# Phase tables for eight pairs at a time, five input buffers, T4 by one difference, output units in two kinds of banks

## The chip, the cores and the metric

The kernel runs on one core of a Trainium2 chip. The metric is the time of one execution in microseconds of the device. The core has five engines with a queue of instructions each, which they run in order: TensorE (PE: matmuls and transposes), VectorE (DVE), ScalarE (ACT), GpSimd (POOL) and SyncE (SP, which here only issues DMAs). An instruction waits until all that it needs is there, and all behind it on its engine wait with it.

## The reference

One layer on x of shape (1, 2048, 1024), float32:

```python
h = rms_norm(x, norm_g)
proj = einsum('bsd,dc->bsc', h, w_in)             # 10240 columns
(ssm_u, ssm_gate, ret_q, ret_k, ret_v, ret_gate, diff_q, diff_k, diff_v, diff_gate,
 mem_q, mem_gate, merge) = split(proj)             # 12 pieces of 512, merge 4 x 1024
a_out = s5_branch(ssm_u, ...) * silu(ssm_gate)     # diagonal complex state, 32 groups
b_out = retention_branch(ret_q, ret_k, ret_v, ...) * silu(ret_gate)
c_out = diff_attn_branch(diff_q, diff_k, diff_v, ...) * silu(diff_gate)
m_out = memory_branch(mem_q, rms_norm(mem, mem_norm_g), ...) * silu(mem_gate)
br = einsum('bsnc,ncd->bsnd', stack(a_out, b_out, c_out, m_out), w_branch)
merged = sum(sigmoid(merge + b_merge) * br, axis=branch)
out = x + einsum('bsd,de->bse', merged, w_out)
```

In the S5 branch a state of group g runs with a = exp((lr + i li) dt), where dt = exp(log_dt).

## The kernel before

The 2048 tokens are two blocks b of 1024. In each block the stages follow one another: retention (32 units of a head and a token tile), differential attention, `projections`, `merge_output` (merging, the memory branch, the S5 output) and `output`. A float32 product is made of three: each factor is split into a high and a low half, x = xh + xl (names that end in h and l), and xh wh, xl wh and xh wl are summed in one bank of PSUM. A high half is a cast on ACT, a low half a subtraction on DVE or POOL. Apart from `projections`, whose order is written out by hand, a scheduler arranges the instructions of a stage for every engine, led by the due times with which code is put in (`ev.at`), and then each engine keeps that order.

**Input tiles** (`Norm`, L560 to L590). A tile of 128 tokens is loaded (`n_x`, L569), scaled (`n_junk` on ACT, `rms_m` on DVE, `rms_r` on POOL, `n_x` on DVE, L579) and transposed in two halves (PE, L586), then split into `xh` and `xl`. Block 0 has three buffers for it. Tiles 0 and 1 go first, the other six stand beside the first retention units, and the loads of the small parameter vectors (`vst`, `gqk`, `ldt_r`, `lt`) between them.

**S5 tables** (`setup_s5`, L308 to L440). Alongside retention of block 0, for four of 16 pairs of groups at a time (four blocks j0), the powers a^1 to a^128 are built by doubling (`tab`, products in `big`), brought to magnitude one and stored (`mats_d`). Then follow the matrices `gm` (transposed by PE at L372), `ca` (L426) and `tpad`. Retention's own instructions on DVE, `rsm` (L923: masked scores) and the rotations `ram` and `rbm`, stand in the same queue. The generator is advanced in 198 slots, one for each `yield`.

**T4** (`x_mix`, L1382 to L1407). `projections` multiplies by a scheme of seven products s instead of eight for a pair of column blocks (a `Pair`), on combinations of the four quarters of the block's input: T1, T2, T3 and T4 = B(0, 1) - T2, each for k = 0..3 and each split. Product s has 12 matmuls (L1355) into bank "abcbadc"[s]; `prepare` makes the weights' combinations and splits (`p_h`, `p_l`) ahead of it, and `collect` (`p_t`) takes banks over on DVE or ACT. T4 is used by product 5, and formed during products 0 to 3 of the first pair (`late`).

**Output** (L1543 to L1575). 16 units of 24 matmuls: `o = ps_mm()`, a bank of a pool of two; the sum with x (`mg_t`, L1572) releases it. The units' left factors `w1h` and `w1l` are eight pieces of 128x128 for each token tile.

Of the kernel before, what the change touches and what calls it, by code (L numbers as in the profile page):

```python
# [11 lines left out]
F32 = mybir.dt.float32  # L12
# [8 lines left out]
D = 1024  # L21
# [22 lines left out]
def trunk_kernel(ctx, tc, a):  # L44
# [135 lines left out]
    def setup_s5(p):  # L180
# [127 lines left out]
        dT = p.tile([16, 32], F32, name="dT")  # L308
        V.tensor_copy(dT, pt[0:16, 0:32])
        m = 4  # L310
        for j0 in range(0, n, m):
            yield
            js = slice(j0, j0 + m)
            big = [p.tile([128, m * 9 * 16], F32, name=f"big{i}") for i in range(2)]

            tab = p.tile([128, m, 2, 128], F32, name="tab")
            V.tensor_copy(tab[:, :, 0, 0], e_r[:, js])
            V.tensor_copy(tab[:, :, 1, 0], e_i[:, js])
            for q in (1, 2, 4, 8, 16, 32, 64):
                tmp = [bg[:, 0:m * q].rearrange("p (j c) -> p j c", j=m) for bg in big]  # L320
                cmul(tab[:, :, 0, q:2 * q], tab[:, :, 1, q:2 * q],
                     (tab[:, :, 0, 0:q], tab[:, :, 1, 0:q]),
                     (bc(tab[:, :, 0, q - 1], 2, q), bc(tab[:, :, 1, q - 1], 2, q)), tmp)
                yield
            tmp = [bg[:, 0:m * 128].rearrange("p (j c) -> p j c", j=m) for bg in big]
            tt(tmp[1], tab[:, :, 1, :], tab[:, :, 1, :], ALU.mult, G)
            yield
# [50 lines left out]
                DMA.dma_start(out=mats_d[:, j0 + j:j0 + j + 2, 0:256], in_=ev)  # L378
                yield

            cm = p.tile([16, 2, 2 * m, 64], F32, name="cm")
            for i, nm in enumerate(("ssm_c_re", "ssm_c_im")):
                DMA.dma_start(out=cm[:, i], in_=a[nm][0].rearrange("g h p -> h g p")[:, 2 * j0:2 * j0 + 2 * m, :])
            cT = p.tile([128, 2, m, 16], F32, name="cT")
# [31 lines left out]
                                  in_=ca[r0:r0 + 64, i, :, 1:9, :].rearrange("p j s h -> p j (s h)"))  # L416
                yield

            tpad = p.tile([16, m, 2, 256], F32, name="tpad")
            V.memset(tpad[:, :, :, 0:128], 0.0)  # L420
            for g2 in range(2):
                pt = ps_tr()
                r0 = g2 * 64
                for j in range(m):
                    for i in range(2):
                        PE.matmul(pt[0:16, j * 128:(j + 1) * 128], bb[r0:r0 + 64, i, j, :],  # L426
                                  ca[r0:r0 + 64, i, j, 0:8, :].rearrange("p s h -> p (s h)"),
                                  start=i == 0, stop=i == 1)
                V.tensor_copy(tpad[:, :, g2, 128:256], pt[0:16, :].rearrange("p (q c) -> p q c", q=m))
# [3 lines left out]
            tv = tpad.rearrange("p j g c -> p (j g) c")  # L433
            tt(tv[:, :, 128:144], tv[:, :, 128:144], dd, ALU.add)
            for s in range(8):
                for g2 in range(2):
                    DMA.dma_start(out=mats_d[s * 16:(s + 1) * 16, js, 512 + g2 * 128:640 + g2 * 128],
                                  in_=tpad[:, :, g2, 128 - 16 * s:256 - 16 * s])
                if s % 4 == 3:
                    yield  # L440

# [118 lines left out]
    class Norm:  # L560
# [818 lines left out]
    def x_mix(b, k, xs, xm):  # L1379

        (x0h, x0l), (x1h, x1l) = xT[b, 0], xT[b, 1]

        def raw(h, l, j, name, bufs):
            t = xm.tile([128, 512], F32, name=name, bufs=bufs)
            V.tensor_tensor(t, h[:, j, :].bitcast(F32), l[:, j, :].bitcast(F32), op=ALU.add)
            return t

        def split(t, d):
            A.copy(d[0][:, k, :], t)
            yield  # L1390
# [12 lines left out]
        yield from split(t1, xs["t1"])
        t4 = raw(x0h, x0l, 4 + k, "x_c", 2)
        V.tensor_tensor(t4, t4, xs["t2"][0][:, k, :].bitcast(F32), op=ALU.subtract)
        V.tensor_tensor(t4, t4, xs["t2"][1][:, k, :].bitcast(F32), op=ALU.subtract)
        yield from split(t4, xs["t4"])  # L1407

    def projections(b, mg, first):
# [4 lines left out]
        with pool("xs") as xsp, pool("pw") as pw, pool("pe") as pe, tc.manual_schedule(engines=ORDERED):  # L1414
# [114 lines left out]
    def output(b, mg, gp, norms):  # L1529
        merged, w1 = mg.merged, mg.w1  # L1530
        units = [(eh, t) for eh in range(2) for t in range(8)]
        for i, (eh, t) in enumerate(units):
# [90 lines left out]
    for b in range(NBLK):  # L1623
# [118 lines left out]
```

## Time and profile before

| | |
|---|---|
| median of 3 runs | 3001.69 us (2997.6 to 3002.18) |
| profiled execution | 3003.64 us, span of its trace 3001.9 us |
| mean granted clock of PE | 0.987 |
| PE busy | 2871.8 us, 96% of the span |
| DVE, ACT, POOL busy | 65%, 44%, 39% |

The span is the time from the first to the last instruction in the trace of one execution; the profiled execution's own time is 1.7 us longer. A granted clock of 1 is 2.4 GHz, of 0.5 it is 1.2 GHz; a value between them is a mean over a stretch.

### The profile page before, as it was taken

How to read it: one execution, taken by the hardware profiler on the slowest of the kernel's cores; microseconds unless marked ns; L12 is line 12 of the kernel's file. 1: busy time of each engine (PE TensorE's matmuls, PEld its weight loads, DVE VectorE, ACT ScalarE, POOL GpSimd, SP SyncE). 2: the span in 40 equal slices, each digit the busy share in tenths (PEclk: the TensorE clock that was granted, in tenths of full speed). 3: DMA queues.
4: the chain of work that ended last, by engine and by line, in shares of the span. 5: the costliest groups of instructions: out<-in, count | busy, mean ns of one | idle time of the engine just before them, and what ended most of it. 6: DMA issues, size and time to landing. Idle time of an engine off the chain costs nothing.

```text
span 3001.9 us, 42940 instructions
## 1 busy us (share of the span) xinstructions
PE 2871.8 (96%) x14258; PEld 2374.7 (79%) x14258; DVE 1937.6 (65%) x4658; ACT 1315.2 (44%) x3365; POOL 1171.2 (39%) x1121
## 2 busy tenths in 40 slices
PE   7898999998999999999999999999999999999999
PEld 6777777777888888787788878878877888888787
DVE  7785487767656545676543378888876655446664
ACT  4223355563333344523433357777743333344322
POOL 3443544423444443643132242332224444445450
PEclk9899999999999999999999999999999999999999
DMA  4443422223444437664521220220224445366642
GB/s 139 103 99 86 123 68 71 71 81 119 145 156 142 135 121 237 186 197 148 157 70 37 64 70 20 64 63 17 64 74 156 146 139 160 126 199 184 203 154 93
DMA packets 319644, 351.74 MB, mean 117 GB/s; under 512 B 26735, under 2 KB 238782, under 8 KB 319422
## 3 DMA queue, kind: packets, MB, share of 16 engines
q1 hardware_dynamic: 317118, 340.60, 36.6%
q0 software_dynamic: 2304, 8.39, 0.9%
q8 instruction: 113, 1.85, 0.3%
q14 instruction: 109, 0.89, 0.1%
HBM read 247.99 MB, written 100.93 MB: 116 GB/s over the span
## 4 chain that ended last, share of the span: by engine, by line
PE 72%; DVE 13%; POOL 4%; ACT 4%; DMA 3%; issue 3%; SPq 0%; POOLq 0%; ACTq 0%; DVEq 0%
PE sc L1355 15%; PE mm L75 8%; PE mm L77 8%; PE mm L76 8%; PE mm L1355 7%; PE tr L1355 4%; PE sc L76 3%; PE sc L75 3%; PE sc L77 3%; PE o L818 3%; POOL rms_r L139 2%; PE tr L809 1%; DVE nm L768 1%; PE sc L764 1%; PE sc L763 1%
## 5 line engine op out<-in xcount | busy, mean ns | idle before, releaser
L1317 POOL TENSOR_TENSOR p_l<-p_r,p_h 128x512 fp32r<-128x512 f32 x256 | 349.3, 1372 | 497.8 <-ACT p_h L1316 497.8
L75 PE MATMUL mm<-w5h,xh 128*128 128x512 f32 x1024 | 438.0, 428 | 6.9 <-ACT xh L589 2.7
L76 PE MATMUL mm<-w5l,xh 128*128 128x512 f32 x1024 | 408.3, 399 | 3.1 <-POOL w5l L455 3.1
L77 PE MATMUL mm<-w5h,xl 128*128 128x512 f32 x1024 | 409.4, 400 | 0.0
L139 POOL TENSOR_TENSOR rms_r<-rms_m,mhalf 128x1 f32<-128x1 f32 (+1 forms) x228 | 175.9, 773 | 509.0 <-DVE rms_m L137 445.0
L1316 ACT CAST p_h<-p_r 128x512 fp32r<-128x512 f32 x260 | 155.8, 616 | 293.2 <-DVE p_r L1341 225.7
L770 ACT ACTIVATE pr<-sc,nm 128x512 f32<-128x512 f32 (+3 forms) x320 | 200.1, 626 | 149.0 <-DVE nm L768 147.5
L77 PEld LDWEIGHTS mm<-w5h,xl 128*128 128x128 f32 x1024 | 195.5, 191 | 43.9 <-issue 0.4
L75 PEld LDWEIGHTS mm<-w5h,xh 128*128 128x128 f32 x1024 | 196.5, 192 | 37.3 <-ACT xh L589 3.1
L76 PEld LDWEIGHTS mm<-w5l,xh 128*128 128x128 f32 x1024 | 196.9, 192 | 31.6 <-POOL w5l L455 3.9
L76 PE MATMUL sc<-br_l,w1h 128*128 128x512 f32 x496 | 196.5, 396 | 7.5 <-DVE br_l L1234 7.5
L75 PE MATMUL sc<-br_h,w1h 128*128 128x512 f32 x496 | 199.7, 403 | 2.9 <-ACT br_h L1233 2.9
L768 DVE TENSOR_REDUCE nm<-sc 128x1 f32<-128x512 f32 (+3 forms) x320 | 193.4, 605 | 9.1 <-PE sc L764 5.1
L77 PE MATMUL sc<-br_h,w1l 128*128 128x512 f32 x496 | 195.9, 395 | 0.0
L818 PEld LDWEIGHTS o<-vt,at 128*128 128x128 f32 x1088 | 141.9, 192 | 38.0 <-ACT at L811 29.5
L472 POOL TENSOR_TENSOR w1l<-w_r,w1h 128x512 fp32r<-128x512 f32 x86 | 116.7, 1360 | 139.1 <-ACT w1h L471 135.7
L818 PE MATMUL o<-vt,at 128*128 128x128 f32 x1088 | 151.3, 279 | 17.0 <-ACT at L811 17.0
L455 POOL TENSOR_TENSOR w5l<-w_r,w5h 128x512 fp32r<-128x512 f32 x72 | 97.1, 1352 | 114.8 <-ACT w5h L454 76.6
L1438 ACT ACTIVATE p_t<-p_t,vec 128x512 f32<-128x512 f32 x96 | 69.5, 724 | 157.8 <-DVE p_t L1367 75.7
L1289 POOL TENSOR_TENSOR mg<-mg,mg_g 128x512 f32<-128x512 f32 x64 | 93.7, 1468 | 111.8 <-DVE mg_g L1288 88.0
L1355 PE MATMUL mm<-xh,p_h 128*128 128x512 f32 x336 | 133.8, 398 | 0.0
L1355 PE MATMUL mm<-xh,p_l 128*128 128x512 f32 x336 | 131.2, 390 | 1.4 <-POOL p_l L1317 1.4
(401 smaller groups left out, 7698.0 us busy)
## 6 DMA issues: line engine op xcount, KB each, us to landing
p_r<-in_w_in SPq DMA_DIRECT2D x88, 512.0 KB
w_r<-in_w_in SPq DMA_DIRECT2D x144, 256.0 KB
me_d<-p_t SPq DMA_DIRECT2D x128, 256.0 KB
mg_g<-me_d SPq DMA_DIRECT2D x64, 512.0 KB
s_m<-mats_d SPq DMA_DIRECT2D x32, 640.0 KB
w_r<-in_w_branch SPq DMA_DIRECT2D x64, 256.0 KB
b_r<-br SPq DMA_DIRECT2D x52, 256.0 KB
n_x<-in_x SPq DMA_DIRECT2D x16, 512.0 KB
```

The costliest lines, as they stand in the source:

```text
L75: PE.matmul(out, l[0], r[0], start=first, stop=False)
L76: PE.matmul(out, l[0], r[1], start=False, stop=False)
L77: PE.matmul(out, l[1], r[0], start=False, stop=last)
L139: G.tensor_tensor(r, m, mhalf[:, 0:n], op=ALU.pow)
L455: (V if k % 2 else G).tensor_tensor(lo, raw, hi.bitcast(F32), op=ALU.subtract)
L472: G.tensor_tensor(lo, raw, hi.bitcast(F32), op=ALU.subtract)
L768: V.tensor_reduce(nm, s[:, 0:n], axis=AX.X, op=ALU.max, negate=True)
L770: A.activation(e[:, 0:n], s[:, 0:n], AF.Exp, bias=nm, accum_out=self.zz[:, m, c:c + 1])
L818: PE.matmul(self.o[:, 0:128], self.at[c][:, q * 128:(q + 1) * 128], self.st["vts"][c][:, q, :], start=c == 0 and q == 0, stop=c * 4 + q == ...
L1316: A.copy(hi, x)
L1317: eng.tensor_tensor(lo, x, hi.bitcast(F32), op=ALU.subtract)
L1355: PE.matmul(o, l[:, k, :], r, start=first and k == 0 and q == 0, stop=k == 3 and q == 2, skip_group_check=True)
```

## The change

1. **Tables for eight pairs.** `tabs` holds eight pairs and is doubled in blocks 0 and 2 only; a block takes its half. The products go to `wide`, which has the buffer of `gm`. More yields stand between the instructions (18 for a table of eight, where a table of four had 7). `tpad` is two tiles, the second in the buffer of `cm`.
2. **Input tiles.** Five buffers instead of three; the load of tile 3 stands ahead of all, and the small vectors come at 2.5 in place of 0.3.
3. **T4.** POOL sums the quarter's two halves, and DVE takes T2 off as it was before it was split, where it took off T2's halves one after the other. `late` makes two sums at a time.
4. **Output.** Odd units take a bank of the pool `sc`.

```diff
+        n8 = 8
         for j0 in range(0, n, m):
...
-            tab = p.tile([128, m, 2, 128], F32, name="tab")
...
-                cmul(tab[:, :, 0, q:2 * q], tab[:, :, 1, q:2 * q],
-                     (tab[:, :, 0, 0:q], tab[:, :, 1, 0:q]),
-                     (bc(tab[:, :, 0, q - 1], 2, q), bc(tab[:, :, 1, q - 1], 2, q)), tmp)
-                yield
+            if j0 % n8 == 0:
+                tabs = p.tile([128, n8, 2, 128], F32, name="tabs")
...
+                wide = p.tile([128, 2, n8 * 64], F32, name="wide", tag="tab")
+                for q in (1, 2, 4, 8, 16, 32, 64):
+                    u, w = [wide[:, i, 0:n8 * q].rearrange("p (j c) -> p j c", j=n8) for i in range(2)]
...
+                    tt(u, x[0], y[0], ALU.mult)
+                    tt(w, x[1], y[1], ALU.mult)
+                    if q > 16:
+                        yield
+                    tt(tabs[:, :, 0, q:2 * q], u, w, ALU.subtract)
+                    yield
...
+            tab = tabs[:, j0 % n8:j0 % n8 + m]
...
-            tpad = p.tile([16, m, 2, 256], F32, name="tpad")
+            tpads = [p.tile([16, m, 256], F32, name="tpad0"), p.tile([16, m, 256], F32, name="tpad1", tag="cm")]
...
-            self.x = self.p.tile([128, D], F32, name="n_x", bufs=(3, 2)[b])
+            self.x = self.p.tile([128, D], F32, name="n_x", bufs=(5, 2)[b])
...
-        b22 = raw(x1h, x1l, 4 + k, "x_c", 2)
-        t2 = xm.tile([128, 512], F32, name="x_f", bufs=2)
+        t2 = raw(x1h, x1l, 4 + k, "x_c", 4)
         V.tensor_tensor(t1, b12, t1, op=ALU.subtract)
...
-        t4 = raw(x0h, x0l, 4 + k, "x_c", 2)
-        V.tensor_tensor(t4, t4, xs["t2"][0][:, k, :].bitcast(F32), op=ALU.subtract)
-        V.tensor_tensor(t4, t4, xs["t2"][1][:, k, :].bitcast(F32), op=ALU.subtract)
+        t4 = xm.tile([128, 512], F32, name="x_b", bufs=4)
+        G.tensor_tensor(t4, x0h[:, 4 + k, :].bitcast(F32), x0l[:, 4 + k, :].bitcast(F32), op=ALU.add)
+        yield
+        V.tensor_tensor(t4, t4, t2, op=ALU.subtract)
         yield from split(t4, xs["t4"])
...
             for g in range(LEAD):
                 prepare(g)
+                if g % 2:
+                    step(g - 1, g)
             plain(1, 0)
-            late = {0: (0, 0), 1: (1, 1), 2: (2, 2), 3: (3, 3)}
+            late = {0: (0, 1, 0, 1), 1: (2, 2), 2: (3, 3)}
...
-            o = ps_mm()
+            o = ps_sc() if i % 2 else ps_mm()
...
-                    ev.at(0.3, setup_vectors, np_)
+                    norms[3].load()
+                    ev.at(2.5, setup_vectors, np_)
...
-                        if i < 5:
-                            ev.at(i, norms[i + 3].load)
+                        if i < 4:
+                            ev.at(i, norms[i + 4].load)
```

The order of instructions changes in the retention stage of block 0, at T4 in both projection stages, and in the output only by the banks' names.

SP's queue near its start, from the small vectors to the next loads, before:

```order
L152 DMA vst<-in_ssm_b_glu 4x128
L152 DMA vst<-in_mem_q_norm_g 1x128
L152 DMA vst<-in_mem_k_norm_g 1x128
L152 DMA vst<-in_ssm_lambda_re 16x128
L152 DMA vst<-in_ssm_lambda_im 16x128
L152 DMA vst<-in_diff_head_norm_g 1x128
L159 DMA gqk<-in_diff_q_norm_g 128x64
L160 DMA gqk<-in_diff_k_norm_g 128x64
L164 DMA ldt_r<-in_ssm_log_dt 128x32
L169 DMA lt<-in_diff_lambda_q 128x64 x2
L169 DMA lt<-in_diff_lambda_k 128x64 x2
L569 DMA n_x<-in_x 128x1024 x3
```

and now, from the third load on (the lines of the code are 16 to 18 further down):

```order
L585 DMA n_x<-in_x 128x1024
L460 DMA w_r<-in_w_in 128x4x128 x4
L976 DMA rtab<-in_c_rrope 128x8x256
L978 DMA rmask<-in_c_rmask 128x512
L585 DMA n_x<-in_x 128x1024 x4
L152 DMA vst<-in_mem_norm_g 8x128
L152 DMA vst<-in_b_merge 32x128
L152 DMA vst<-in_ssm_b_glu 4x128
```

Four loads of input tiles stand ahead of the small vectors, where there was one, with three behind them.

DVE's queue, the end of the first table's doubling (`big` are the products, 128x256 the last), before:

```order
L187 TENSOR_TENSOR tab<-big_1186,big_1187 128x4x16
L187 TENSOR_TENSOR big_1186<-tab 128x128
L187 TENSOR_TENSOR big_1187<-tab 128x128
L187 TENSOR_TENSOR tab<-big_1186,big_1187 128x4x32
L187 TENSOR_TENSOR big_1186<-tab 128x128
L187 TENSOR_TENSOR big_1187<-tab 128x128
L455 TENSOR_TENSOR w5l<-w_r,w5h 128x512
L187 TENSOR_TENSOR tab<-big_1186,big_1187 128x4x32
L923 TENSOR_TENSOR rsm<-sc,rmask 128x128
L187 TENSOR_TENSOR big_1186<-tab 128x256
L187 TENSOR_TENSOR big_1187<-tab 128x256
L455 TENSOR_TENSOR w5l<-w_r,w5h 128x512
```

and now (the last doubling, 128x512):

```order
L187 TENSOR_TENSOR wide<-tabs 128x512 x2
L471 TENSOR_TENSOR w5l<-w_r,w5h 128x512
L939 TENSOR_TENSOR rsm<-sc,rmask 128x128
L187 TENSOR_TENSOR tabs<-wide 128x8x64
L913 SCALAR_TENSOR_TENSOR ram<-mm,rdec,rtab 128x128 x2
L913 SCALAR_TENSOR_TENSOR rbm<-mm,rdec,rtab 128x128 x2
L187 TENSOR_TENSOR wide<-tabs 128x512
L640 SCALAR_TENSOR_TENSOR rg<-si_t,mm 128x128
L187 TENSOR_TENSOR wide<-tabs 128x512
L956 SCALAR_TENSOR_TENSOR state<-state,sc 128x128
L654 TENSOR_TENSOR on<-sc,rg 128x128
L187 TENSOR_TENSOR tabs<-wide 128x8x64
```

The instructions are twice as wide, and retention's stand between them. Counted in PE's order, the first transposes of `gm` of the four blocks stand at 379, 564, 739 and 905 before, and at 415, 579, 771 and 934 now.

DVE's queue while the first pair's products run in block 0, k = 0 and 1 of T4, before (L1385 the sum, L1405 and L1406 the differences, L1391 the low half, L1364 a collection):

```order
L1385 TENSOR_TENSOR x_c<-xh,xl 128x512
L1405 TENSOR_TENSOR x_c<-x_c,x_t2h 128x512
L1406 TENSOR_TENSOR x_c<-x_c,x_t2l 128x512
L1391 TENSOR_TENSOR x_t4l<-x_c,x_t4h 128x512
L1364 TENSOR_TENSOR p_t<-sc,p_t 128x512
L1385 TENSOR_TENSOR x_c<-xh,xl 128x512
L1405 TENSOR_TENSOR x_c<-x_c,x_t2h 128x512
L1406 TENSOR_TENSOR x_c<-x_c,x_t2l 128x512
L1391 TENSOR_TENSOR x_t4l<-x_c,x_t4h 128x512
```

and now (L1422 the difference, L1407 the low half, L1380 the collection):

```order
L1343 TENSOR_TENSOR p_s<-p_r 128x512
L1345 TENSOR_TENSOR p_r<-p_r 128x4x128
L1346 TENSOR_TENSOR p_r<-p_s,p_r 128x4x128
L1422 TENSOR_TENSOR x_b<-x_b,x_c 128x512 x2
L1407 TENSOR_TENSOR x_t4l<-x_b,x_t4h 128x512 x2
L1380 TENSOR_TENSOR p_t<-sc,p_t 128x512
L1422 TENSOR_TENSOR x_b<-x_b,x_c 128x512
L1407 TENSOR_TENSOR x_t4l<-x_b,x_t4h 128x512
```

The sum and one difference are gone; the collection stands behind two differences and two low halves, where it stood behind one T4. POOL's queue at the same place, before:

```order
L472 TENSOR_TENSOR w1l<-w_r,w1h 128x512 x2
L139 TENSOR_TENSOR rms_r<-rms_m,mhalf 128x1 x4
L1317 TENSOR_TENSOR p_l<-p_r,p_h 128x512 x4
L1317 TENSOR_TENSOR p_l<-p_s,p_h 128x512
L1317 TENSOR_TENSOR p_l<-p_r,p_h 128x512 x6
```

and now (L1420 the sum):

```order
L139 TENSOR_TENSOR rms_r<-rms_m,mhalf 128x1 x4
L1333 TENSOR_TENSOR p_l<-p_r,p_h 128x512 x4
L1420 TENSOR_TENSOR x_b<-xh,xl 128x512 x2
L1333 TENSOR_TENSOR p_l<-p_s,p_h 128x512
L1333 TENSOR_TENSOR p_l<-p_r,p_h 128x512
L1420 TENSOR_TENSOR x_b<-xh,xl 128x512 x2
L1333 TENSOR_TENSOR p_l<-p_r,p_h 128x512 x5
```

Two sums stand ahead of the third product's `p_l`, and two ahead of the fifth's.

## Rows read from the trace of the kernel before

**Rows 1.** the page, its busy times and the chain that ended last
```profile
PE 2871.8 (96%) x14258; PEld 2374.7 (79%) x14258; DVE 1937.6 (65%) x4658; ACT 1315.2 (44%) x3365; POOL 1171.2 (39%) x1121
...
PE 72%; DVE 13%; POOL 4%; ACT 4%; DMA 3%; issue 3%; SPq 0%; POOLq 0%; ACTq 0%; DVEq 0%
```

**Rows 2.** waits of PE: line, releaser, us in total, times, longest us
```profile
PE tr L1355 <- ACT x_t4h L1389: 11.8, 4, 5.0
...
PE tr L372 <- DVE gm L187: 8.6, 5, 2.7
...
PE sc L931 <- DVE rsm L923: 6.3, 4, 3.8
...
PE tr L586 <- DVE rms_m L137: 4.8, 1, 4.8
...
PE mm L75 <- DVE mg_t L1572: 3.6, 2, 3.2
...
PE tr L426 <- DVE ca L187: 3.5, 3, 1.5
```

**Rows 3.** timeline of PE: start us, duration us, instruction, [idle before <- releaser]
```profile
158.09 0.57 PE L372 MATMUL tr<-ident,gm 128*128 128x128 f32 x2 [2.66 <-DVE gm L187]
...
240.68 0.44 PE L372 MATMUL tr<-ident,gm 128*128 128x128 f32 x2 [2.19 <-DVE gm L187]
...
244.14 0.87 PE L372 MATMUL tr<-ident,gm 128*128 128x128 f32 x6 [1.62 <-DVE gm L187]
...
728.52 0.80 PE L1355 MATMUL tr<-x_t4h,p_h 128*128 128x512 f32 x1 [4.99 <-ACT x_t4h L1389]
...
1401.32 0.80 PE L75 MATMUL mm<-br_h,w1h 128*128 128x512 f32 x1 [3.22 <-DVE mg_t L1572]
```

**Rows 4.** windows: length, busy us (instructions) by engine, PEclk, DMA share, GB/s
```profile
40.00:50.00 10.00, 7.29 (x34) 6.39 (x35) 8.17 (x24) 4.21 (x10) 2.37 (x4) 0.83 0.33 84
80.00:90.00 10.00, 6.17 (x31) 5.03 (x30) 9.90 (x24) 5.37 (x13) 6.11 (x6) 0.83 0.63 183
110.00:120.00 10.00, 8.52 (x30) 6.36 (x31) 4.84 (x14) 1.99 (x7) 5.22 (x5) 0.52 0.11 33
725.00:730.00 5.00, 1.48 (x3) 0.95 (x4) 4.11 (x8) 0.62 (x1) 0.00 (x0) 0.50 0.62 165
730.00:735.00 5.00, 5.00 (x20) 4.04 (x19) 1.89 (x3) 2.67 (x5) 3.62 (x3) 0.83 0.40 150
1400.00:1405.00 5.00, 3.69 (x9) 2.92 (x10) 4.45 (x11) 1.95 (x6) 0.68 (x1) 0.57 0.67 199
1405.00:1410.00 5.00, 5.00 (x18) 3.98 (x17) 1.47 (x8) 1.15 (x6) 0.00 (x0) 0.75 0.61 225
```

**Rows 5.** timeline of DVE while T4 is formed, block 0
```profile
713.00 1.66 DVE L1405 TENSOR_TENSOR x_c<-x_c,x_t2h 128x512 f32<-128x512 f32 x1
...
717.05 0.69 DVE L1391 TENSOR_TENSOR x_t4l<-x_c,x_t4h 128x512 fp32r<-128x512 f32 x1 [0.69 <-ACT x_t4h L1389]
```

**Rows 6.** timeline of POOL in the same stretch
```profile
710.68 5.13 POOL L1317 TENSOR_TENSOR p_l<-p_r,p_h 128x512 fp32r<-128x512 f32 x3
```

**Rows 7.** timeline of DVE at the third output unit, block 0
```profile
1390.59 7.99 DVE L1559 SCALAR_TENSOR_TENSOR w1l<-mg,w1h 128x128 fp32r<-128x128 f32 x12
...
1400.57 0.69 DVE L1572 TENSOR_TENSOR mg_t<-mm,mg_t 128x512 f32<-128x512 f32 x1
```

**Rows 8.** timeline of SP's queue, the loads behind the small vectors
```profile
27.63 6.08 SPq L569 DMA_DIRECT2D n_x<-in_x  x3
```

**Rows 9.** groups by line and form, 0 to 330 us: busy us, mean ns | idle
```profile
L187 DVE TENSOR_TENSOR big<-tab 128x256 f32<-128x256 f32 x16 | 6.5, 439 | 0.1
...
L187 DVE TENSOR_TENSOR tab<-big,big 128x256 f32<-128x256 f32 x8 | 3.4, 422 | 0.0
...
L187 DVE TENSOR_TENSOR big<-tab 128x512 f32<-128x512 f32 x4 | 3.2, 790 | 0.1
...
L187 DVE TENSOR_TENSOR big<-tab 128x4 f32<-128x4 f32 x16 | 2.0, 160 | 0.1
```

More of the change, by code (lines that the diff above doesn't have):

```diff
@@ L314, in setup_s5 @@
             big = [p.tile([128, m * 9 * 16], F32, name=f"big{i}") for i in range(2)]
-            tab = p.tile([128, m, 2, 128], F32, name="tab")
[L317 to L320, printed above, removed]
-                cmul(tab[:, :, 0, q:2 * q], tab[:, :, 1, q:2 * q],
-                     (tab[:, :, 0, 0:q], tab[:, :, 1, 0:q]),
-                     (bc(tab[:, :, 0, q - 1], 2, q), bc(tab[:, :, 1, q - 1], 2, q)), tmp)
-                yield
+            if j0 % n8 == 0:
+                tabs = p.tile([128, n8, 2, 128], F32, name="tabs")
+                V.tensor_copy(tabs[:, :, 0, 0], e_r[:, j0:j0 + n8])
+                V.tensor_copy(tabs[:, :, 1, 0], e_i[:, j0:j0 + n8])
+                wide = p.tile([128, 2, n8 * 64], F32, name="wide", tag="tab")
+                for q in (1, 2, 4, 8, 16, 32, 64):
+                    u, w = [wide[:, i, 0:n8 * q].rearrange("p (j c) -> p j c", j=n8) for i in range(2)]
+                    x = tabs[:, :, 0, 0:q], tabs[:, :, 1, 0:q]
+                    y = bc(tabs[:, :, 0, q - 1], 2, q), bc(tabs[:, :, 1, q - 1], 2, q)
+                    tt(u, x[0], y[0], ALU.mult)
[4 more added lines that the diff above has]
+                    yield
+                    tt(u, x[0], y[1], ALU.mult)
+                    tt(w, x[1], y[0], ALU.mult)
+                    if q > 16:
+                        yield
+                    tt(tabs[:, :, 1, q:2 * q], u, w, ALU.add)
+                    yield
+            tab = tabs[:, j0 % n8:j0 % n8 + m]
             tmp = [bg[:, 0:m * 128].rearrange("p (j c) -> p j c", j=m) for bg in big]
@@ L379, in setup_s5 @@
                 yield
-            cm = p.tile([16, 2, 2 * m, 64], F32, name="cm")
+            cm = p.tile([16, 2, 2 * m, 64], F32, name="cm", tag="cm")
             for i, nm in enumerate(("ssm_c_re", "ssm_c_im")):
@@ L417, in setup_s5 @@
                 yield
-            tpad = p.tile([16, m, 2, 256], F32, name="tpad")
-            V.memset(tpad[:, :, :, 0:128], 0.0)
+            tpads = [p.tile([16, m, 256], F32, name="tpad0"), p.tile([16, m, 256], F32, name="tpad1", tag="cm")]
+            for tpad in tpads:
+                V.memset(tpad[:, :, 0:128], 0.0)
             for g2 in range(2):
@@ L428, in setup_s5 @@
                                   start=i == 0, stop=i == 1)
-                V.tensor_copy(tpad[:, :, g2, 128:256], pt[0:16, :].rearrange("p (q c) -> p q c", q=m))
+                V.tensor_copy(tpads[g2][:, :, 128:256], pt[0:16, :].rearrange("p (q c) -> p q c", q=m))
                 yield
@@ L432, in setup_s5 @@
             tt(dd, bc(dT[:, 2 * j0:2 * j0 + 2 * m], 2, 16), bc(ident[0:16, 0:16], 1, 2 * m), ALU.mult)
-            tv = tpad.rearrange("p j g c -> p (j g) c")
-            tt(tv[:, :, 128:144], tv[:, :, 128:144], dd, ALU.add)
+            for g2 in range(2):
+                tv = tpads[g2][:, :, 128:144]
+                tt(tv, tv, dd.rearrange("p (j g) c -> p j g c", g=2)[:, :, g2, :], ALU.add)
             for s in range(8):
@@ L437, in setup_s5 @@
                     DMA.dma_start(out=mats_d[s * 16:(s + 1) * 16, js, 512 + g2 * 128:640 + g2 * 128],
-                                  in_=tpad[:, :, g2, 128 - 16 * s:256 - 16 * s])
+                                  in_=tpads[g2][:, :, 128 - 16 * s:256 - 16 * s])
                 if s % 4 == 3:
@@ L1395, in x_mix @@
         b12 = raw(x1h, x1l, k, "x_b", 4)
-        b22 = raw(x1h, x1l, 4 + k, "x_c", 2)
-        t2 = xm.tile([128, 512], F32, name="x_f", bufs=2)
+        t2 = raw(x1h, x1l, 4 + k, "x_c", 4)
         V.tensor_tensor(t1, b12, t1, op=ALU.subtract)
-        V.tensor_tensor(t2, b22, t1, op=ALU.subtract)
-        V.tensor_tensor(b12, b22, b12, op=ALU.subtract)
+        V.tensor_tensor(b12, t2, b12, op=ALU.subtract)
+        V.tensor_tensor(t2, t2, t1, op=ALU.subtract)
         yield from split(t2, xs["t2"])
@@ L1403, in x_mix @@
         yield from split(t1, xs["t1"])
[L1404 to L1406 removed]
+        t4 = xm.tile([128, 512], F32, name="x_b", bufs=4)
+        G.tensor_tensor(t4, x0h[:, 4 + k, :].bitcast(F32), x0l[:, 4 + k, :].bitcast(F32), op=ALU.add)
+        yield
+        V.tensor_tensor(t4, t4, t2, op=ALU.subtract)
         yield from split(t4, xs["t4"])
```

## Prediction

> **What bounds the kernel now.** I read the page first: TensorE (PE) is busy 2871.8 us of a span of 3001.9, and the chain that ended last runs 72% on PE and 13% on VectorE (DVE) [rows 1]. The change adds no matmul and removes none, so all it can win is idle time of PE, 130 us in all, and matmuls run at the lower clock. Next I read what PE waited for [rows 2]: six kinds of wait there belong to three places that the change touches. (a) The first retention stage, about 0 to 380 us: 4.8 us for the fourth input tile, 8.6 and 3.5 us for the S5 tables (gm, ca), 6.3 us for retention's masked scores (rsm), which stand in DVE's queue among the table work. (b) The products with T4 in both projection stages, 11.8 us. (c) The third output unit of block 0, most of 3.6 us. PE's timeline shows the places [rows 3], and the windows show that PE's clock falls from 2.4 to 1.2 GHz around such gaps: the mean grant is 0.83, 0.52, 0.50 and 0.57 where PE is busy 7.29 of 10, 8.52 of 10, 1.48 of 5 and 3.69 of 5 us [rows 4]. A gap therefore costs itself and part of the microseconds behind it.
>
> **T4.** Before, DVE ran four 128x512 instructions for each k (sum, two differences, low half). Now GpSimd (POOL) forms the sum, and DVE has one difference and the low half. A DVE instruction of that size takes 0.69 us alone, and 1.66 us where POOL runs its own [rows 5]; three of POOL's took 5.13 us, 1.71 each, in the same stretch [rows 6], so the two engines hold each other up. DVE's path to the last T4 becomes shorter by 2 x 0.69 to 2 x 1.66 us for each k, 5.5 to 13 us over four, more than the 5.0 us for which PE waits. But the order shows what the four sums are put in front of. POOL makes p_l(2) behind two sums and p_l(4) behind two more, and PE's third product needs p_l(2): 1.5 us by the 1.71, which takes the place of p_l waits that PE has there already, so I count 0. The collection of product 1 stands on DVE behind two differences and two low halves. The second difference can't begin before POOL's second sum, which ends 2 x 1.71 = 3.4 us behind the p_l before it. Product 3 overwrites the bank that this collection reads; with some 0.7 us of slack, PE waits 2.4 us. Product 6 waits another 0.8 for collection 3 (one 128x512 instruction ahead of it). Per block: the x_t4h waits are 11.8 / 2 = 5.9 us; the clock lost around the last is (1 - 0.50) x 1.48 + (1 - 0.83) x 5.00 = 1.6 [rows 4]; less 2.4 and 0.8, it is 4.3 us. Two blocks: **8.6 us**. Bounds: 15 if the new waits don't come (2 x 7.5); 4 if p_l(2) costs its 1.5 in full and a new gap of 2 us costs 0.8 of clock (2 x 2.0).
>
> A rule of the Trainium skill speaks against this edit: in "SBUF — State Buffer" (Who interferes with whom) a VectorE instruction with two SBUF inputs and a GpSimd instruction that reads SBUF exclude each other for their whole length. Of the new sums each would then hold VectorE up for its length. The 1.66 beside the 0.69 agrees with that. By the rule the block gives 4.3 us, without it up to 7.5.
>
> **Output units.** Unit 3 of block 0 waits at 1401.32 for unit 1's sum (3.22 us), because the pool of mm banks holds two and that sum, an instruction of 0.69 us, stands on DVE behind 12 low halves that take 7.99 us [rows 3, 7]. With odd units in the sc banks unit 3 needs a bank that has long been free. What it needs next is late by nothing that I can find: all but the last of its low halves are made within the 7.99 us, by 1398.6, about when PE falls idle (1398.1). The clock lost behind it is (1 - 0.57) x 3.69 + (1 - 0.75) x 5.00 = 2.8 us [rows 4]. So 3.2 + 2.8, and 0.4 in block 1 (3.6 - 3.2 [rows 2]), are 6.4; for a low half that is a little late I take off 0.4: **6.0 us** (bounds 3 and 6.4). DVE's order stays the same.
>
> **Retention 0, the start.** Five input buffers let tile 4 load while PE is at tile 2, and the order puts four n_x loads before the small vectors where three stood behind them. The 4.8 us wait goes, and (1 - 0.83) x 7.29 = 1.2 us of clock [rows 2, 4], **6.0 us**. The price: the small vectors, and the whole chain to the phase table with them, move behind these loads. Issuing three such loads took 6.08 us including their wait for buffers [rows 8], so the chain is later by anything from some 1 to 6 us; I take 3.5.
>
> **Retention 0, the tables.** Before, each of four blocks doubled its own table in 42 instructions: 14 groups from 128x4 to 128x256, 42.6 us busy in all, 10.65 for each block (the first of them and the last two of each kind stand in [rows 9]). Now there are two tables with 42 instructions of twice the width. Widths 8 to 256 priced at the same rows (busy over count), and 512 at 0.80, make 14.5 us for one, 29.0 for both. DVE saves 13.6 us, but unevenly: blocks 1 and 3 have 3.9 us more before their gm, blocks 2 and 4 have 10.65 less. Two smaller edits, tpad in two halves and its buffer shared with cm, change one add and one memset for two each and move a load that is needed much later: nothing.
>  - Block 1: gm is ready 3.9 + 3.5 = 7.4 us later in DVE's work. PE's order has its transposes 36 instructions further back, some 8 us of matmuls, so PE needn't wait longer than before; but DVE is busy 9.90 of 10 us just ahead [rows 4], so rsm instructions come later too. Of the 6.0 won at the start I keep 4.5.
>  - Block 2: gm has 10.65 us less work ahead. The 2.66 us wait goes [rows 3], and with a ca wait (3.5 in three) and the clock I count 4.0.
>  - Block 3: 3.9 more work, with little waited there before: a loss of 0.7.
>  - Block 4: two waits of 2.19 and 1.62 [rows 3] go: 3.8.
> Together 4.5 + 4.0 - 0.7 + 3.8 = **11.6 us**. Bounds: a loss of 8 (DVE is the limit, blocks 1 and 3 pay 7.4 + 3.9, the start's gain is waited away again and blocks 2 and 4 win 3 only) and a gain of 31 (all waits of (a) in rows 2 gone, 23 us, and some 8 us of clock).
>
> **Sum.** 8.6 + 6.0 + 11.6 = 26.2 us from the profiled execution's 3003.6 gives 2977.4. That execution is 2.0 us above the median of the three runs (3001.7), so I expect a median of about **2975.5 us**, 0.9% faster.
>
> **Rivals.**
>  1. The S5 part returns nothing. For it: DVE at 9.90 of 10 us ahead of the first gm; what the start wins is then waited at rsm and gm. Against it: blocks 2 and 4 have 10 us less of that work. Left are 8.6 + 6.0: 2987.
>  2. All of (a) goes, 23 us and 5 or more of clock, since DVE has 13.6 us less to do: 8.6 + 6.0 + 29 is 43.6, 2958. Against it: the table now comes in two lumps.
>  3. The four sums on POOL do no good: p_l(2) and the collections come as late as T4 did, by the mutual hold-up, and PE waits in other places as long. T4 gives 0: 2984. Against it: the path that carries the last T4 is shorter by at least 5.5 us. The Trainium skill's rule named above is this mechanism taken to its end; the 1.66 bears it out for pairs of instructions, not for the whole stretch.
>  4. Slower: the first lump of table work. If DVE can't hide the 3.9 and 3.5 us ahead of block 1, nor 3.9 of block 3, PE waits for rsm and gm 11.3 us more, with the clock at 0.52 in two windows of 10 us (4.1 lost in each, by 8.52 busy), and the start wins nothing: 11.3 + 8.2 + 3 for other heads is 22.5 lost against 14.6 won: 3010. It decides from a loss of 20.6 in the retention stage (14.6 + 6).
>  5. The banks do nothing, because unit 3 waits for its low halves at the same time: 6.0 less, 2981.5.
>
> **How the numbers follow.** The sum, give or take 7: 0.50. Rival 1: 0.20. Rival 2: 0.10. Rival 3: 0.08. Rival 4: 0.06. Rival 5: 0.06. The forecast is that of the sum, its own range 2969 to 2983. To leave out no more than 2 in 10 the range reaches rival 2 at its end and rival 1 with some loss in the retention stage: 2955 to 2996. Within 0.2% (6 us, about what a measurement of this kernel can tell from no change) lies only rival 1 together with rival 3, or half of rival 4: 0.08. Slower 0.06; faster 0.86.
>
> **What would show it.** In the changed profile: no gap of PE at about 42 us and a clock of 1.00 there; no gm wait in blocks 2 and 4, and a first gm 2 to 6 us later in DVE's queue; the 5.0 us waits for x_t4h gone, with a wait of about 2 us for a collection (p_t) or for p_l in their place; POOL's sums at 1.3 to 1.7 us; no wait for mg_t, and a full clock from 1395 to 1410 (of this trace's times). I would be wrong if PE's waits for rsm in 50 to 120 us grew beyond their 6.3 us, if the scheduler's new order of the whole stage opened a gap in a place that I don't name, or if x_t4h were still waited for.

## The result and the profile after

| | median | range | ratio to the kernel before, 95% interval |
|---|---|---|---|
| before | 3000.05 us | 2997.6 to 3002.18, 4 runs | |
| changed | 2985.16 us | 2983.98 to 2985.94, 4 runs | 0.9947 (0.9935 to 0.9958) |

The change makes the kernel 14.9 us faster. I had forecast faster with a chance of 0.86, 26.2 us less and 2975.5; the time is inside the stated range (2955 to 2996), but it is that of rival 1 (2987), in which the retention stage returns next to nothing. The range holds it because it was widened to take in that rival; the sum's own range, 2969 to 2983, is missed by 2 us. The profiled execution took 2985.94 us.

The page's busy row, as in [rows 1]:

```profile
PE 2869.3 (96%) x14258; PEld 2369.7 (79%) x14258; DVE 1922.9 (64%) x4562; ACT 1315.6 (44%) x3365; POOL 1185.4 (40%) x1129
```

DVE has 96 instructions fewer and POOL eight more. What PE waited for, with the same columns as [rows 2] (lines are 14 to 18 higher than in the kernel before):

```profile
PE tr L386 <- DVE gm L187: 8.7, 7, 2.2
...
PE sc L947 <- DVE rsm L939: 4.8, 3, 2.8
PE sc L75 <- ACT br_h L1249: 4.4, 4, 1.4
PE sc L1371 <- DVE p_t L1380: 4.1, 2, 2.1
PE tr L441 <- DVE ca L191: 3.4, 2, 1.8
...
PE sc L1371 <- POOL p_l L1333: 3.2, 4, 1.1
...
PE tr L441 <- DVE ca L187: 2.8, 2, 1.6
PE mm L75 <- DVE rms_m L137: 2.7, 1, 2.7
...
PE tr L602 <- DVE vec L156: 1.5, 1, 1.5
```

The 11.8 us for x_t4h and the 3.6 us for mg_t of [rows 2] are gone. The 4.8 us for tile 4 became 1.5 us for the small vectors (vec) and 2.7 us for a scaled tile. But gm stands at 8.7 us, where it had 8.6, and ca (both lines) at 6.2. At T4 the wait for p_t is new, and p_l is waited for in two more places. PE's timeline shows where; the columns are those of [rows 3]:

```profile
37.91 0.66 PE L602 MATMUL tr<-ident,n_x 128*128 128x128 f32 x4 [1.47 <-DVE vec L156]
49.10 0.64 PE L75 MATMUL mm<-w5h,xh 128*128 128x512 f32 x1 [2.72 <-DVE rms_m L137]
...
155.37 0.44 PE L386 MATMUL tr<-ident,gm 128*128 128x128 f32 x2 [1.64 <-DVE gm L187]
...
712.55 0.50 PE L1371 MATMUL sc<-xh,p_l 128*128 128x512 f32 x1 [1.14 <-POOL p_l L1333]
717.18 0.47 PE L1371 MATMUL sc<-x_t3h,p_h 128*128 128x512 f32 x1 [2.06 <-DVE p_t L1380]
```

Windows of the changed kernel, as in [rows 4]:

```profile
20.00:360.00 340.00, 312.11 (x1582) 249.35 (x1581) 231.04 (x683) 109.60 (x332) 142.29 (x145) 0.95 0.38 102
140.00:150.00 10.00, 10.00 (x53) 8.37 (x52) 4.83 (x15) 3.66 (x13) 3.75 (x6) 1.00 0.54 103
715.00:720.00 5.00, 2.94 (x10) 2.29 (x10) 4.32 (x5) 0.62 (x1) 5.00 (x4) 0.83 0.00 0
720.00:725.00 5.00, 5.00 (x20) 4.03 (x19) 4.31 (x4) 1.75 (x3) 3.72 (x3) 0.83 0.37 112
1390.00:1395.00 5.00, 5.00 (x24) 4.14 (x23) 4.32 (x11) 3.39 (x11) 2.44 (x3) 1.00 1.02 347
1395.00:1400.00 5.00, 5.00 (x24) 4.14 (x23) 4.50 (x12) 3.55 (x14) 0.68 (x1) 1.00 0.69 215
```

In 20 to 360 us PE is idle 27.9 us (340 - 312.11). The kernel before has 31.7 there:

```profile
20.00:360.00 340.00, 308.30 (x1581) 248.27 (x1580) 238.23 (x761) 110.19 (x332) 141.45 (x145) 0.96 0.39 102
```

DVE works 7.2 us less in that stretch (238.23 to 231.04), PE stands still 3.8 us less, and the mean clock is 0.95 after 0.96. In the same 340 us PE runs as many matmuls as before (1582 and 1581): what it no longer waits it loses at the lower clock. The differential attention behind this stage begins with the transposes of `kn`, and they start at the same time before (L722) and now (L738):

```profile
361.94 0.49 PE L722 MATMUL tr<-ident,kn 128*128 128x128 f32 x3
361.84 0.93 PE L738 MATMUL tr<-ident,kn 128*128 128x128 f32 x4
```

One profile of each could be chance. But in the three profiles of this study with the retention stage as before these transposes start at 361.3 to 362.4 us, and in the four with the stage as changed at 357.7 to 362.9, 361.3 on average. So the change returns about 1 us there, where I had forecast 11.6. The output stage of block 0 shows no gap and a full clock.

### The profile page after: what moved, and what is told of

Its sections match the earlier page's. It is cut to its first block, busy times and chain, and to the rows that moved or that the text cites. A ratio compares the mean times of both kernels' runs of the same rounds, so it can differ in the third digit from the quotient of the medians.

```text
span 2984.2 us, 42821 instructions
## 1 busy us (share of the span) xinstructions
PE 2869.3 (96%) x14258; PEld 2369.7 (79%) x14258; DVE 1922.9 (64%) x4562; ACT 1315.6 (44%) x3365; POOL 1185.4 (40%) x1129
## 4 chain that ended last, share of the span: by engine, by line
PE 47%; DVE 4%; ACT 1%; issue 1%; POOL 1%; DMA 1%; SPq 0%; POOLq 0%; ACTq 0%; DVEq 0%
PE sc L1371 7%; PE mm L75 5%; PE mm L77 5%; PE mm L76 5%; PE mm L1371 4%; PE sc L76 3%; PE sc L75 3%; PE sc L77 3%; PE o L834 2%; PE tr L1371 2%; PE tr L825 1%; PE sc L779 1%; PE sc L780 1%; DVE nm L784 1%; DMA w_r<-in_w_in 1%
## 5 line engine op out<-in xcount | busy, mean ns | idle before, releaser
L76 PE MATMUL sc<-br_l,w1h 128*128 128x512 f32 x624 | 246.3, 395 | 6.0 <-DVE br_l L1250 6.0
L75 PE MATMUL sc<-br_h,w1h 128*128 128x512 f32 x624 | 249.9, 400 | 2.3 <-ACT br_h L1249 2.3
L77 PE MATMUL sc<-br_h,w1l 128*128 128x512 f32 x624 | 245.6, 394 | 0.0
L76 PEld LDWEIGHTS sc<-br_l,w1h 128*128 128x128 f32 x624 | 118.4, 190 | 29.2 <-DVE br_l L1250 7.2
L75 PEld LDWEIGHTS sc<-br_h,w1h 128*128 128x128 f32 x624 | 118.8, 190 | 25.2 <-ACT br_h L1249 3.1
L77 PEld LDWEIGHTS sc<-br_h,w1l 128*128 128x128 f32 x624 | 118.4, 190 | 25.2
```

The costliest lines, as they stand in the source:

```text
L75: PE.matmul(out, l[0], r[0], start=first, stop=False)
L76: PE.matmul(out, l[0], r[1], start=False, stop=False)
L77: PE.matmul(out, l[1], r[0], start=False, stop=last)
```

## The experiments

All times are medians, with the kernel before run on the same chip beside them; the difference is that of the two medians, and the ratio with its interval is worked out from all runs, so that the two can differ by some 1.5 us. Each kernel computes the whole reference. My theory after the result was that the matmul stages had paid as forecast and the retention stage had not, because what stands in its way there is no lack of DVE's time.

### Each part by itself

The kernel before with one part of the change each. Of the diff above these are the pieces on `tabs`, `wide` and `tpads`; those on `n_x`, on the loads and on 2.5; those on `x_mix`, the steps between `prepare` and `late`; and the one line of the output. In short:

```diff
+                tabs = p.tile([128, n8, 2, 128], F32, name="tabs")
```

```diff
-            self.x = self.p.tile([128, D], F32, name="n_x", bufs=(3, 2)[b])
+            self.x = self.p.tile([128, D], F32, name="n_x", bufs=(5, 2)[b])
```

```diff
+        V.tensor_tensor(t4, t4, t2, op=ALU.subtract)
```

```diff
-            o = ps_mm()
+            o = ps_sc() if i % 2 else ps_mm()
```

Expected of the tables:

> The kernel before with the tables for eight pairs (and the two halves of tpad) alone. Theory A: the waits for gm and ca are set by chains of single results and by where PE's order puts the transposes, not by how much work DVE has; DVE is relieved of some 10 us and PE's waits for gm stay within 2 us of their 8.6: no change, 2997 to 3003. Theory B: the tables gain 5 to 8 us by themselves, and the changed start takes it away again: 2992 to 2996, with the gain standing at 270 us of the trace.

Of the start:

> The kernel before with five input buffers, the early load of tile 3 and the later small vectors alone. Theory A: the 4.8 us wait for tile 4 goes and others of 3 to 5 us come in 35 to 50 us of the trace, for the small vectors and for a scaled tile: no change, 2998 to 3003. Theory B: without the longer first table the start keeps 4 to 6 us: 2994 to 2996.

Of T4:

> The kernel before with T4 by one difference and its sums on POOL alone. From the trace of the change, where the two projection stages are 2.6 and 3.5 us shorter: 6 us less, 2994, with a wait of 2.1 us for the collection of product 1 in each block. By the prediction's term 8.6 us less: 2991.5. If the trace of the change had shown only chance: 3000.

Of the banks:

> The kernel before with output units in two kinds of banks alone. From the trace of the change: 6 to 7 us less, 2993.5, nearly all of it between the first and the fourth output unit of block 0. If unit 3 waits for its low halves instead, 0 to 2 less.

| before 3000.89 us, 31 runs | median, 10 runs each | less | ratio, 95% interval |
|---|---|---|---|
| tables | 2998.00 us | 2.9 | 0.9990 (0.9977 to 1.0003) |
| start | 2995.14 us | 5.8 | 0.9976 (0.9966 to 0.9985) |
| T4 | 2994.43 us | 6.5 | 0.9981 (0.9972 to 0.9991) |
| banks | 2995.97 us | 4.9 | 0.9980 (0.9971 to 0.9989) |

T4 came out as read from the trace of the change; the banks came out 1 to 2 us under it, which their interval (3.3 to 8.7 us) allows. With the start neither theory was wholly right: it gains by itself (B), though the waits that I named for A came, 1.4 and 2.7 us in its profile where 4.8 stood:

```profile
PE mm L75 <- DVE rms_m L137: 2.7, 1, 2.7
...
PE tr L586 <- DVE vec L156: 1.4, 1, 1.4
```

The tables' gain can't be told from nothing, as A had it. Their gm waits are 7.8 us:

```profile
PE tr L386 <- DVE gm L187: 7.8, 6, 2.2
```

The four differences add up to 20.1 us; the whole change has 15. By an estimate from the spread of these runs the sum may lie anywhere from 15 to 26 us, so this alone does not show that the parts don't add up.

### The parts taken out of the change, more distance, and the sums earlier

Four kernels on one chip, with the kernel before at 3000.56 us. The first is the changed kernel itself.

> The changed kernel again, for the comparison with the others of this series on one chip: 15 us below the kernel before, 2985 to 2987.

It took 2985.25 us, ratio 0.9948 (0.9933 to 0.9963). The second has the tables of before (the diff of the tables, undone):

> The changed kernel with the tables of before (four pairs at a time, whole tpad). Theory A (the parts of the retention stage don't add up; what DVE saves there isn't on PE's path): within 3 us of the changed kernel. Theory B (the tables win some 7 us net as in my forecast, 3.9 lost and 10.6 relieved in turn): 6 to 8 us slower than the changed kernel.

2983.56 us, 0.9942 (0.9927 to 0.9957): no slower than with the new tables. A holds; the 6 to 8 us of B are not there. Its gm waits are larger (11.7 us), and its PE is yet as idle as with the new tables (28.2 us):

```profile
20.00:360.00 340.00, 311.77 (x1594) 250.61 (x1593) 237.69 (x768) 110.65 (x335) 144.12 (x149) 0.96 0.38 103
```

The third puts PE's readers further behind the chains that they read:

```diff
             tt(gm[:, 1], tmp[0], tmp[1], ALU.add)
             yield
             yield
             yield
+            yield
+            yield
...
             ts(ca[:, 1], tmp[0], -1.0, ALU.mult)
             yield
             yield
+            yield
+            yield
```

> The changed kernel with two more yields ahead of the gm transposes and two ahead of the ca matmuls in each block, so that PE's instructions stand some 1.6 us of other work further back. Theory A (gm and ca come at the pace of the slots, as a chain of single results of some 6 us, and PE's order puts the readers too early): PE's waits for gm and ca, 14.9 us, fall by half or more; 4 to 10 us faster than the changed kernel. Theory C (DVE lacks throughput there): the waits stay within 3 us, no change.

2985.06 us, 0.9954 (0.9939 to 0.9969): no change. In its profile gm falls from 8.7 to 1.5 us, but ca to 4.1 only, and other waits have grown, among them one for the memory branch's setup (L525):

```profile
PE sc L951 <- DVE rsm L943: 6.2, 5, 2.9
...
PE tr L445 <- DVE ca L191: 4.1, 2, 3.0
...
PE tr L525 <- DVE rms_m L137: 2.3, 2, 1.6
PE tr L388 <- DVE gm L187: 1.5, 1, 1.5
```

```profile
20.00:360.00 340.00, 313.97 (x1562) 251.16 (x1561) 223.29 (x677) 109.54 (x329) 141.21 (x140) 0.93 0.38 101
```

PE is idle 26.0 us, 2 to 3 less than in the changed kernel, and the mean clock in this stretch is 0.93. The profiled execution is the slowest of the five (2992.56 us). So the place of the readers does decide the gm wait, as A says against C, and removing it bought no time, against A.

The fourth moves POOL's sums for k = 0 and 1 ahead of the second product's p_l:

```diff
             for g in range(LEAD):
                 prepare(g)
-                if g % 2:
-                    step(g - 1, g)
+                if g in (0, 3):
+                    step(*((0, 1) if g == 0 else (2, 3)))
```

> The changed kernel with POOL's first two sums ahead of the second product's p_l instead of behind it, where POOL stands idle for 2.8 us; the other two stay behind the fourth p_l. Theory P (POOL's place in the queue makes the new waits): the wait of 2.1 us for the collection and that for p_l of product 2 (1.1) go in both blocks, with some clock: 6 to 8 us faster than the changed kernel. Theory L (DVE and POOL hold each other up for whole instructions, wherever they stand): the waits move and the time stays within 2 us.

2985.56 us, 0.9944 (0.9922 to 0.9966; four runs from 2977.3 to 2989.0): no change that can be told, as theory L has it. The old waits shrank, and a new one stands in front of product 1, for p_h (PE's timeline):

```profile
710.62 0.50 PE L1371 MATMUL sc<-x_t2h,p_h 128*128 128x512 f32 x1 [2.01 <-ACT p_h L1332]
```

Its cause is in DVE's timeline: the two differences of weights that p_h is cast from now run beside POOL's sums and take 1.66 and 1.57 us:

```profile
706.57 1.66 DVE L1345 TENSOR_TENSOR p_r<-p_r 128x512 f32<-128x512 f32 x1
708.34 1.57 DVE L1346 TENSOR_TENSOR p_r<-p_s,p_r 128x512 f32<-128x512 f32 x1
```

### The sums on DVE, and the start taken out

```diff
-        G.tensor_tensor(t4, x0h[:, 4 + k, :].bitcast(F32), x0l[:, 4 + k, :].bitcast(F32), op=ALU.add)
+        V.tensor_tensor(t4, x0h[:, 4 + k, :].bitcast(F32), x0l[:, 4 + k, :].bitcast(F32), op=ALU.add)
```

> The changed kernel with the four sums of T4 on DVE instead of POOL; T4 still by one difference. In the trace of the change DVE stands idle for 3.3 us in front of the first two differences, waiting for POOL's sums, and POOL's p_l of product 2 waits behind them. Theory P (the new waits come from the two sums in POOL's queue): the wait for p_l of product 2 (1.1 us) and the collection's 2.1 us go, 4 to 8 us faster than the changed kernel, 2977 to 2981. Theory L (what T4 costs DVE decides, and 0.7 to 1.7 us more for each k come back as waits for x_t4h): 0 to 4 us slower.

2984.92 us against 3000.73, 0.9947 (0.9932 to 0.9962): the same as with POOL's sums. Theory P's number did not come, and theory L's, 0 to 4 us slower, can't be told from it. Of the waits at T4 that for p_l fell, and that for the collection stayed:

```profile
PE sc L1371 <- DVE p_t L1380: 4.8, 2, 2.4
...
PE sc L1371 <- POOL p_l L1333: 1.6, 2, 0.9
```

The other kernel has three buffers and the early small vectors of before, with all else changed.

```diff
-            self.x = self.p.tile([128, D], F32, name="n_x", bufs=(5, 2)[b])
+            self.x = self.p.tile([128, D], F32, name="n_x", bufs=(3, 2)[b])
...
-                    norms[3].load()
-                    ev.at(2.5, setup_vectors, np_)
+                    ev.at(0.3, setup_vectors, np_)
...
```

> The changed kernel with three input buffers and the early small vectors of before. If the start's gain of 5.8 us, measured alone, stands beside the new tables: 2989 to 2992. If the longer first table takes it away (rival 1 of the prediction): 2984 to 2987.

2984.50 us, 0.9940 (0.9921 to 0.9958). With the new tables the start brings nothing that can be measured, as rival 1 of the prediction has it. The four runs spread from 2979.0 to 2989.3 us, so a gain of some 4 us is not ruled out.

### Distance once more, so that nothing is pushed back

The changed kernel with the tables of before and all the yields of the third kernel above, and the changed kernel with its two yields ahead of gm alone (before 3003.12 us on this chip).

> The changed kernel with the tables of before, and two more yields ahead of the gm transposes and of the ca matmuls in each block: 189 of the 198 slots, where the same yields with the new tables took 197 and pushed the memory branch's setup back. Theory A (the waits for gm and ca belong to PE's order, and their removal counts if nothing is pushed back): those waits, 15.7 us with the old tables, fall below 6, and the time is 4 to 10 us under the changed kernel, 2975 to 2981. Theory D (what is won in one place of this stage is waited or lost to the clock in another, as in the four kernels before): idle time of PE in the first 360 us stays at 38 to 41 us, and the time within 3 us of 2984.

2994.45 us, 0.9969 (0.9957 to 0.9982): 8.7 us less than the kernel before, where the same kernel without the yields had 17.0 on its chip. Two of its six runs took 2987 us and four 2994 to 2995.5; the profile is of one of the two, so what the others lose is not seen. The gm and ca waits, 13.5 us in that profile, did not fall below 6.

> The changed kernel with two more yields ahead of the gm transposes alone, 189 of 198 slots. Theory A: the gm waits of 8.7 us fall below 3, the ca waits stay at 6 to 8, 3 to 6 us under the changed kernel. Theory D: idle time of PE in the first 360 us within 2 us of the changed kernel's 40 to 41, the time within 3 us.

2981.95 us, 0.9925 (0.9913 to 0.9937), the fastest version in this study. But it isn't fast for theory A's reason: gm waits fell to 7.3 us only, and PE's idle time is that of the changed kernel (28.4 us), at a clock of 0.97:

```profile
PE tr L388 <- DVE gm L187: 7.3, 6, 2.6
```

```profile
20.00:360.00 340.00, 311.63 (x1608) 249.76 (x1607) 229.78 (x690) 112.03 (x337) 145.75 (x150) 0.97 0.39 103
```

Its interval ends about where those of the changed kernel begin, so that it beats it is likely and not shown.

## Why the prediction was right, and where not

**Output: right.** 6.0 us forecast, 4.9 measured alone (interval 3.3 to 8.7). In the two traces the matmuls between the first unit and the fourth of block 0 take 6.3 us less, and that is the gap of [rows 3] and the clock of [rows 4], which is back at 1.00 in the windows above.

**T4: the mechanism right, the size 2 us too large.** 8.6 forecast, 6.5 measured alone. The waits for x_t4h went, and the collection costs 2.06 us where I had 2.4. The traces show the size more sharply than the runs. From the first matmul with p_h to the first with w0h, block 0 takes 456.4 to 456.6 us in the four profiles without the new T4 and 453.7 to 453.9 in the eight with it as changed; block 1 takes 454.9 to 455.4 and 451.2 to 451.3. That is 2.7 and 3.8 us, 6.5 together. Two terms were too good. The clock: I counted 1.6 us per block as won, but the new wait lowers it as the old one did, by (1 - 0.83) x 2.94 + (1 - 0.83) x 5.00 = 1.35 us in the windows above. And the wait for product 2's p_l (1.14) does not take the place of others, as I had it: the p_l waits were 3.0 us over both blocks before (1.6 and 1.4 in the view of [rows 2]) and are 4.0 with it (3.2 and 0.8). One was too bad: the 0.8 for collection 3 did not come, so that collections cost 4.1 us over both blocks in place of 6.4. With these 8.6 becomes 8.6 - 2.7 - 1.0 + 2.3 = 7.2. Rival 3 did not come either.

That the sums are on POOL is worth nothing by itself: with them on DVE the time is the same, and earlier on POOL also. In the traces they even cost a little there: the two stretches take 451.7 and 450.3 us with the sums on DVE and 452.6 and 450.1 with two of them earlier, 3.0 and 2.3 us less together (one profile each; the medians can't tell it). What pays is then that T2 is taken off in one instruction and not in two, or the new order of T4's steps that came with it; no run separates these two. POOL and DVE hold each other up wherever the sums stand; the rows of DVE and POOL in the changed kernel show a pair of differences at 1.7 us each beside POOL's work:

```profile
709.61 3.43 DVE L1422 TENSOR_TENSOR x_b<-x_b,x_c 128x512 f32<-128x512 f32 x2 [3.29 <-POOL x_b L1420]
```

```profile
708.29 2.54 POOL L1420 TENSOR_TENSOR x_b<-xh,xl 128x512 f32<-128x512 f32 x2
710.78 1.72 POOL L1333 TENSOR_TENSOR p_l<-p_s,p_h 128x512 fp32r<-128x512 f32 x1
```

POOL's two sums take 1.27 us each; DVE stands idle for the first and begins its first difference just after the second has begun. POOL's p_l takes 1.72 beside the differences. The rule of the Trainium skill named in the prediction ("SBUF — State Buffer", Who interferes with whom) agrees with that, and with the 1.66 and 1.57 us above.

**The start: the size about right alone, nothing with the tables.** 4.5 forecast, 5.8 alone, 0 when taken out of the change (2984.50 against 2985.25, with the spread given above). The place of the loss was named: the small vectors and the chain behind them are later, and PE waits 1.5 us for them. That 2.7 us would follow for a scaled tile was not. So the sign that I had named, no gap at about 42 us and a clock of 1.00 there, came only in part: in 40 to 50 us PE is busy as long as before (7.29 in [rows 4]), with the gap at 46 to 49 us and a clock of 0.96 for 0.83.

```profile
40.00:50.00 10.00, 7.28 (x38) 5.76 (x37) 5.50 (x24) 3.05 (x9) 6.82 (x6) 0.96 0.08 14
```

**The tables: this step failed.** I put 4.0 us on block 2 and 3.8 on block 4, because "gm has 10.65 us less work ahead" and their waits would go; for block 1 I had "PE needn't wait longer than before", and 0.7 us lost for block 3. The sum of PE's waits for gm hardly moved, but its parts did. Before, blocks 1 to 4 had 1.3, 2.7, 0.9 and 3.8 us; blocks 2 and 4 stand in [rows 3], the other two are:

```profile
112.59 0.90 PE L372 MATMUL tr<-ident,gm 128*128 128x128 f32 x3 [1.29 <-DVE gm L187]
...
201.36 0.88 PE L372 MATMUL tr<-ident,gm 128*128 128x128 f32 x6 [0.88 <-DVE gm L187]
```

Now they have 2.9, 2.2 (1.64 in the result's rows, and 0.56), 2.0 and 1.6:

```profile
114.34 0.33 PE L386 MATMUL tr<-ident,gm 128*128 128x128 f32 x1 [0.69 <-DVE gm L187]
116.86 0.55 PE L386 MATMUL tr<-ident,gm 128*128 128x128 f32 x3 [2.20 <-DVE gm L187]
...
157.97 0.87 PE L386 MATMUL tr<-ident,gm 128*128 128x128 f32 x6 [0.56 <-DVE gm L187]
...
201.89 0.44 PE L386 MATMUL tr<-ident,gm 128*128 128x128 f32 x2 [2.02 <-DVE gm L187]
...
243.80 0.44 PE L386 MATMUL tr<-ident,gm 128*128 128x128 f32 x2 [0.88 <-DVE gm L187]
246.33 0.88 PE L386 MATMUL tr<-ident,gm 128*128 128x128 f32 x6 [0.69 <-DVE gm L187]
```

The relieved blocks 2 and 4 won 2.7 us of their 6.5, and blocks 1 and 3, which now carry the tables, lost as much. The waits for ca rose from 4.5 us (3.5 in [rows 2] and the 1.0 below) to 6.2:

```profile
PE tr L426 <- DVE ca L191: 1.0, 2, 0.5
```

A size was off as well. I counted 29.0 us of DVE for doubling both tables; its 14 groups (`wide` and `tabs` at L187) are busy 33.4 us, so blocks 1 and 3 have 6.0 us more ahead of their gm and not 3.9.

Why did the relief win so little? Ahead of block 2's gm DVE had time to spare. In 140 to 150 us it is busy 4.83 of 10 us (8.25 in the next 10 us, in which gm's own chain runs), and yet PE waits for gm at 155.37. Before, it had time there too: the 9.90 of 10 us that I had read [rows 4] stands ahead of block 1's gm. The window of before that goes with the 4.83:

```profile
140.00:150.00 10.00, 10.00 (x51) 8.28 (x50) 5.69 (x17) 2.34 (x9) 3.67 (x5) 1.00 0.51 98
```

DVE's timeline ahead of the wait at 155.37, in the changed kernel:

```profile
150.81 0.84 DVE L471 TENSOR_TENSOR w5l<-w_r,w5h 128x512 fp32r<-128x512 f32 x1 [1.08 <-ACT w5h L470]
151.58 0.28 DVE L939 TENSOR_TENSOR rsm<-sc,rmask 128x128 f32<-128x128 f32 x1
151.78 0.21 DVE L187 TENSOR_TENSOR big<-fi,bi 128x64 f32<-128x64 f32 x1
...
154.62 0.69 DVE L187 TENSOR_TENSOR gm<-big,big 128x512 f32<-128x512 f32 x1 [0.73 <-POOL big L187]
...
157.24 0.68 DVE L187 TENSOR_TENSOR gm<-big,big 128x512 f32<-128x512 f32 x1
```

The first products for gm begin at 151.78, behind a w5l for which DVE waited 1.08 us, and the two halves of gm come 3.5 and 6.1 us later (155.31 and 157.92), with a wait for POOL between. So block 2's gm came 2.7 us sooner than before (PE's first transpose at 155.37 after 158.09), where both blocks together have some 4.6 us less to double ahead of it (21.3 before, 16.7 now); and PE came to it 1.7 us sooner too. Its work is put in at the pace of the yields, behind retention's instructions, and then it is a chain over DVE and POOL of its own length. In a queue that runs in order, time that DVE has left over ahead of an instruction does not bring that instruction forward when it stands behind others that wait. I had read a wait for DVE as a lack of DVE's time. Measured for the tables: 2.9 us alone (not clear of nothing), and 1.7 us the wrong way when taken out of the change. The waits for rsm, by which rival 4 would have shown, fell from 6.3 to 4.8 us. That the tables return nothing is shown; that the chain and the place in the queue are the reason is read from this one stretch, and the run that moved the readers back (gm waits from 8.7 to 1.5 us, no time won) shows that these waits were not worth their length either.

**The sum.** T4 and the banks alone make 11.4 of the 15 us, against 14.6 forecast; start and tables together leave 3.6, against 11.6. By the traces T4 and the banks make 6.5 and 6.3, and the retention stage about 1.

**What stays open.** In the retention stage PE's idle time from 20 to 360 us is 31.7 us before and between 26.0 and 30.7 in the eleven profiles with one or another part of the stage changed, whichever of its waits was removed; most of what goes comes back in another wait. What sets that amount (the sum of the chains, or the order that the scheduler makes of them) no run here separates. Nor is it shown whether start and tables, the first with 5.8 us alone and the second with 2.9 at the edge of what can be told, truly fail to add up, and if so why.

## What to carry to other kernels

A wait for an engine is not yet a lack of that engine's time. Before pricing the relief, look whether the engine is busy up to the instruction that is waited for, and what stands ahead of that in its queue; if it is idle there, or the awaited result is the end of a chain over two engines, less work elsewhere on it may change little: here 2.7 us of 6.5, with as much lost where the work went. Look at such waits place by place, since their sum can stand still while they move. The gap that a bank made was the term nearest to its forecast here, its clock included (6.0 us; 4.9 alone, 6.3 in the traces). Where a wait is replaced by a shorter one, don't count the clock as won.

## What the runs showed of the hardware

TensorE's lower clock comes in other places from run to run of one kernel. The changed kernel, profiled twice, needed 4.1 us less the second time, all of it ahead of 360 us. In 20 to 360 us PE was idle as long (27.9 us, then 28.9), and the mean clock was 0.95, then 0.97. Ahead of 360 us the trace has eight stretches at 1.2 GHz the first time, 30.7 us together, and four the second time, 17.1 us. So differences of some 4 us between single profiles of that stage mean nothing.

Over whole executions the time falls with the mean granted clock. In the 56 runs of the kernel before that stand beside the experiments it is 3005.0 us on average at 0.985 (2 runs), 3002.5 at 0.987 (15), 2999.7 at 0.989 (16) and 2997.7 at 0.990 (6). The clock, which is given to three digits, accounts for about four tenths of the variance of these times; the rest is not explained here.
